# Where the moving operands lie: 256-byte offsets between weights and moving tiles in a hybrid decoder block

## The chip, the cores and the metric

The kernel runs on one core of a Trainium2 chip. The metric is the device time of one execution in microseconds; lower is better. Before the change three runs took 650.53, 650.55 and 651.75 us, a median of 650.55.

## What is computed

One decoder block on a sequence of 1024 tokens and a model width of 1024. After an RMS norm one projection feeds two groups of heads: eight heads of stick-breaking attention (head width 64) and four heads of a gated DeltaNet (head width 128). Both outputs are normed per head, gated, put side by side, and multiplied with one output matrix; the residual is added and normed once more. Cut to what matters here:

```python
h = rmsnorm(x, norm1_w)
proj = einsum('btd,de->bte', h, w_in)
sb_q, sb_k, sb_v, sb_z, g_q, g_k, g_v, g_z, g_b, g_a = split(proj)

# stick-breaking attention, strictly causal, per head
z = einsum('bhqd,bhkd->bhqk', sb_q, sb_k) / sqrt(64)        # scores
attn = where(causal, exp(log_sigmoid(z) - tail), 0)         # tail: sum of softplus(z) behind s
o_sb = rmsnorm(einsum('bhqk,bhkd->bhqd', attn, sb_v)) * silu(sb_z)

# gated delta rule in chunks, per head
o_gdn = rmsnorm(gated_delta_chunked(...)) * silu(g_z)

mixed = concatenate([o_sb, o_gdn], axis=-1)                 # 512 + 512 columns
x = x + einsum('bte,ed->btd', mixed, w_out)                 # output
return rmsnorm(x, final_norm_w)
```

All of it is float32. The change touches where the operands of two products lie, those named scores and output.

## The kernel before

**Products in three parts.** A wide product is made of three matmuls in the float32r type, on operands that are split into a high and a low part: high weights with the high moving operand, high weights with the low one, low weights with the high one (`mm3`, lines 586 to 589). The first argument after the output is the weights (stationary, 128 columns), the next is the moving operand, up to 512 columns. Each matmul instruction brings its own load of weights (LDWEIGHTS), and TensorE loads those of the next matmul while one streams. So the weights that are read during a matmul are those of the next one. In `mm3` two neighbours have the same high weights, and the third has the low ones.

**The stages.** The first stage computes q from the weights `wqh`, `wql` and the normed input `xh`, `xl` (lines 636 to 675). Then come v (`chl` is the moving operand there and `xh`, `xl` are the weights, lines 731 to 735 and 766 to 777), and the other projections (weights `weh`, `wel`, moving `xh`, `xl`, line 937). Attention and the delta rule are woven into the projections: a planner (`Model`, `interleave`) takes steps from several streams by their priorities and by estimated costs of operations, and what it records is the order on each engine. The order on PE is the order of recording. The estimates don't look at addresses.

**Scores.** For each head the planner's stream `attention` loads three tiles (lines 1261 to 1270): `q2` (the high and the low part of q on the two halves of the partitions), `kh` and `kl` (the high and the low part of k, each twice). A `window` then makes blocks of scores: the weights are a slice of 128 columns of `q2`, and `kh` and `kl` are the moving operands, in cuts of at most 512 columns (lines 1300 and 1301). The cuts and the slices begin at multiples of 128 columns, 512 bytes.

**Output.** `product` (lines 1461 to 1478) multiplies a block of 128 tokens, in `mh` and `ml` (the weights, four slices of 128 columns), with the scaled output matrix in `woh0` to `woh7` and `wol0` to `wol7` (moving, 512 columns at a time). It runs twice: first for the delta half (rows 4 to 7 of the matrix, whose tiles are in the pool `f0` on the left), and at the end for the attention half (rows 0 to 3, whose tiles are in the pool `f1` on the right), eight blocks each. The last block of the attention half is cut into 512, 320 and 192 columns.

**Memory.** SBUF is given out from two sides. On the left lie the fixed places (`sg0` to `sg3`, `o2`, `kq`), the constants, and above them, one after another in time, the pools `s0` (first stage), `gd` (delta rule) and `f0` (output). On the right, from the top downwards, lie `att` (attention's tiles, the lowest of which are `kh`, `kl`, `q2`, `v2a`), `pr` (the projections' weights), and under it `px` (`xh`, `xl`), later replaced by `f1`. A pool on the right ends where the one above it begins, so a pool that grows pushes down itself and all that lies under it. Several tags of `att` are used by `chl` tiles of 1040 floats at first, which makes their slots 4160 bytes where `kh` or `kl` need 4096.

The first bytes of the tiles in question, as the compiled program has them:

| tile | first byte | role |
|---|---|---|
| `q2` | 203488 | weights of scores |
| `kh` | 195168 | moving, scores |
| `kl` | 199328 | moving, scores |
| `mh` (three buffers) | 81280, 83328, 85376 | weights of output |
| `ml` (three buffers) | 87424, 89472, 91520 | weights of output |
| `woh4` | 54656 | moving, output, delta half |
| `woh0`, `wol0` | 133728, 137824 | moving, output, attention half |
| `weh` (three buffers) | 180832, 182880, 184928 | weights of the projections |
| `xh`, `xl` | 107104, 139872 | moving, projections |

The pool `gd` ends at byte 106944, 160 bytes below `xh`.

**Small tiles of the delta rule.** `gdn_pre` makes per unit (half a head) the columns `nk`, a root that ScalarE uses a little later (line 1070), and `qe`, which is used at the end of the unit's chain (line 1247).

Of the kernel before, what the change touches and what calls it, by code (L numbers as in the profile page):

```python
# [10 lines left out]
F32 = mybir.dt.float32  # L11
F32R = mybir.dt.float32r
# [5 lines left out]
P = 128  # L18
T = 1024
D = 1024  # L20
NB = T // P
NK = D // P
# [451 lines left out]
def block(tc, xT_d, x_d, n1_d, wE_d, wQ_d, wC_d, conv_d, alog_d, dtb_d, mixw_d, wo_d, fnw_d, out_d):  # L474
# [4 lines left out]
    with ExitStack() as top:  # L479
        top.enter_context(tc.manual_schedule(engines={mybir.EngineType.PE}))  # L480

        def open_pool(name, space="SB", ctx=top, before=(), **kw):
            if space != "SB":
                kw["space"] = getattr(bass.MemoryType, space)
            return Pool(ck, ctx.enter_context(tc.tile_pool(name=name, bufs=1, **kw)), space, before)

        fx = Fixed(ck, nc, {**{f"sg{w}": (2048 * (w + 1), 1) for w in range(4)}, "o2": (1024, 1), "kq": (4096, 4)})
# [52 lines left out]
        at_ = open_pool("att", side="right")  # L540
# [4 lines left out]
        xl = px.tile([P, NK, T], F32R, name="xl")  # L545
        s0_ctx = top.enter_context(ExitStack())
        s0 = open_pool("s0", ctx=s0_ctx)
        n1 = s0.tile([P, NK], F32, name="n1")
        rbc = s0.tile([P, T], F32, name="rbc")

        def turned(tp, parts):
# [65 lines left out]

        chl = []
        for tag, bufs in (("kh", 1), ("kl", 1), ("q2", 1), ("v2a", 1), ("sg2", 1), ("cc", 2), ("cc", 2), ("sg3", 1)):
            chl.append(fx.tile([P, 2, 520], F32R, "chl", tag) if tag[0] == "s" else at_.tile([P, 2, 520], F32R, tag=tag, bufs=bufs, name="chl"))  # L620
        sm = fx.tile([P, 768], F32, "sm", "sg1")
        ones, triu, zero = [sm[:, i * P:(i + 1) * P] for i in range(3)]
        ga = sm[:, 384:448].rearrange("p (b e) -> p b e", e=8)
# [132 lines left out]
        gd = open_pool("gd", ctx=gdn_ctx, before=s0.ops())  # L756
# [198 lines left out]
        def until(name):  # L955
            yield lambda: name in flags
            yield flags[name]


        def delta_pre():  # L960
            yield from decays(pre)
            for h in range(GH):
                for g in range(2):
                    u = 2 * h + g
                    yield from until(f"l{u}g")
                    yield from gdn_pre(h, g)
# [45 lines left out]
        def gdn_pre(h, g):  # L1012
            st = gst[h, g]
            kq = st["kq"]
            cs = slice(4 * g, 4 * g + 4)
            kn = gd.tile([P, 4, P], F32, tag="kn", bufs=4, name="kn")
            ss = gd.tile([P, 2, 4], F32, tag="ss", name="ss")
            cb = gd.tile([P, 4, P], F32, tag="cb", name="cb")
            S.dma_start(cb, cum_s[1, h, cs].partition_broadcast(P))
            dt = gd.tile([P, 4, P], F32, tag="dt", bufs=4, name="dt")  # L1020
            S.dma_start(dt, dt_s[h, g])

            nkv = gd.tile([P, 4, P], F32, tag="nkv", bufs=4, name="nkv")
            kw = fx.words(kq, "kw")
            for which in range(2):
                tp = pz()
                for j in range(4):
                    TE.transpose(tp[:, j * P:(j + 1) * P].bitcast(F32R), kw[:, j, which, :], idr)
                for j in range(4):
                    A.activation(nkv[:, j, :], tp[:, j * P:(j + 1) * P], AF.Square, accum_out=ss[:, which, j:j + 1])  # L1030
                sq = [("A", 250)] * 4
                if which == 0:
                    V.tensor_copy(kn.rearrange("p c d -> p (c d)"), tp)
                    yield
            G.tensor_scalar(ss, ss, EPS, None, ALU.add)
            r2b = gd.tile([P, 4], F32, tag="r2b", bufs=4, name="r2b")
            V.reciprocal(r2b, ss[:, 0, :])
            G.tensor_tensor(r2b, r2b, gsc["beta"][:, h, cs], ALU.mult)
            mr2b = gd.tile([P, 4], F32, tag="mr2b", name="mr2b")
            r = G.tensor_scalar(mr2b, r2b, -1.0, None, ALU.mult)  # L1040
            r2k = gd.tile([P, 4], F32, tag="r2k", bufs=4, name="r2k")
            G.tensor_tensor(r2k, r2b, gsc["kd"][:, h, cs], ALU.mult)
            nk = gd.tile([P, 4], F32, tag="nk", name="nk")
            G.tensor_tensor(nk, ss[:, 0, :], root, ALU.pow)
            qe = gd.tile([P, 4], F32, tag="qe", bufs=4, name="qe")
            G.tensor_scalar(qe, ss[:, 1, :], EPS * P, None, ALU.mult)
            yield r
            nm = dt
            at = gd.tile([P, 4, P], F32, tag="at", bufs=4, name="at")
            for i in range(2):  # L1050
                gpt = pz()
                for j in range(2):
                    c = 2 * i + j
                    TE.matmul(gpt[:, j * 256:(j + 1) * 256], kq[:, c, 0, :], kq[:, c, :, :].rearrange("p a t -> p (a t)"),
                              start=True, stop=True)
                gv = gpt.rearrange("p (j a t) -> p j a t", j=2, a=2)
                V.tensor_tensor(at[:, 2 * i:2 * i + 2, :], gv[:, :, 1, :], dt[:, 2 * i:2 * i + 2, :], ALU.mult)
                for j in range(2):
                    c = 2 * i + j
                    r = V.scalar_tensor_tensor(nm[:, c, :], gpt[:, j * 256:j * 256 + P], mr2b[:, c:c + 1], dt[:, c, :], ALU.mult, ALU.mult)  # L1060
                yield
            st.update(kn=kn, qe=qe, r2b=r2b, r2k=r2k, nkv=nkv, nm=nm, at=at)
            flags[f"p{2 * h + g}"] = r
            yield from until(f"v{2 * h + g}g")
            vt = st["vt"]
            tp = pz()
            for j in range(4):
                TE.transpose(tp[:, j * P:(j + 1) * P].bitcast(F32R), vt[:, j, :], idr)
            for j in range(4):
                A.activation(nkv[:, j, :], tp[:, j * P:(j + 1) * P], AF.Copy, scale=nk[:, j:j + 1])  # L1070
            qg = kq[:, :, 1, :]
            flags[f"q{2 * h + g}"] = G.tensor_tensor(qg, qg, cb, ALU.mult)
            yield
# [180 lines left out]
        def attention():  # L1254
            yield lambda: "v1" in flags and "dec" in flags
            for i in range(2):
                ccs.append(at_.tile([P, T + 1], F32, tag="cc", bufs=2, name="cc"))
                V.memset(ccs[i][:, T:T + 1], 0.0)
            for h in range(SBH):
                yield lambda: f"k{h // 2}" in flags  # L1260
                kh = at_.tile([P, T], F32R, tag="kh", name="kh")
                kl = at_.tile([P, T], F32R, tag="kl", name="kl")
                q2 = at_.tile([P, T], F32R, tag="q2", name="q2")
                i, r = h // 2, slice((h % 2) * 64, (h % 2) * 64 + 64)
                loads = []

                twice = lambda a: a[r, :].unsqueeze(1).to_broadcast([SBD, 2, T])
                for t, src in ((q2, qk_s[i, :, r, :].rearrange("n d t -> d n t")), (kh, twice(qk_s[4 + i, 0])), (kl, twice(qk_s[4 + i, 1]))):
                    loads.append(S.dma_start(t.bitcast(F32), src.bitcast(F32)))
                hd[h] = (q2, kh, kl)  # L1270
                yield loads
                for w in range(4):
                    tok = f"w{w}"
                    yield lambda: busy[tok] == 0 and len([1 for v in busy if v[0] == "w" and busy[v]]) < WINDOWS
                    busy[tok] = 1
                    yield Stream(window(h, w, tok), 10 + 0.01 * (4 * h + w), WINDOW + 0.01 * (4 * h + w))
                    yield lambda: f"s{h}{w}" in flags
            yield lambda: f"e{SBH - 1}3" in flags
# [88 lines left out]
        pools = {}  # L1367
# [145 lines left out]
        def products_attention():  # L1513
            yield lambda: f"d{NB - 1}" in flags
            for b in range(NB):
# [3 lines left out]
                for got in product(b, 0, parts):  # L1519
# [5 lines left out]
                        sy = pools[0].tile([P, 3], F32, tag="sy", bufs=2, name="sy")  # L1525
                        yf = block_tile(0, "yf") if last else y
                    V.tensor_tensor(y[:, hs], yp, y[:, hs], ALU.add)
                    junk = pools[1].tile([P, 512], F32, tag="yj", name="yj")
                    if n == 2:
                        V.scalar_tensor_tensor(junk[:, 0:hs.stop - hs.start], y[:, hs], 1.0 / D, y[:, hs], ALU.mult, ALU.mult, accum_out=sy[:, n:n + 1])  # L1530
                    else:
# [36 lines left out]
                    pre, Stream(delta_load(), 0.4, DELTA + 0.4), Stream(attention(), 9.995, WINDOW), Stream(attention_values(), 9.99, WINDOW), Stream(out_weights(), 9, OUT_WEIGHTS), Stream(out_weights_attention(), 9.25, OUTPUT + 1), Stream(enter_x(), 9.31, OUTPUT), fill,  # L1568
                    Stream(enter_delta(), 9.3, OUTPUT), Stream(prepare(1), 9.2, OUTPUT), Stream(products_delta(), 101, OUTPUT),
                    Stream(enter_attention(), 9.1, OUTPUT - 3), Stream(prepare(0), 9.05, OUTPUT - 2), Stream(products_attention(), 102, OUTPUT - 1.5)])  # L1570

        order = mybir.DependencyInfo(mybir.DependencyClass.NoSync, mybir.DependencyReason.DATA)
# [36 lines left out]
```

## Time and profile before

| | |
|---|---|
| median of three runs | 650.55 us |
| profiled execution | 650.36 us |
| its span, first to last instruction | 648.4 us |
| mean granted TensorE clock | 0.997 |
| matmul and weight-load instructions on PE | 3976 each |
| DMA | 111.82 MB, mean 172 GB/s |

The profile names operands by tiles, with buffer numbers left out, so that all eight `woh` tiles appear as `woh`; the two halves of the output are told apart by time (the delta half up to about 595 us, the attention half behind it). Nearly all operations carry line 358, that of the planner's recorder, so tiles are what tells groups apart. In the groups a matmul's busy time runs from its start to a modelled end, and neighbours overlap; the pace of a stream is read from the distance between starts.

### The profile page before, as it was taken

The numbers are of one execution on the slowest core, as the hardware profiler recorded it, in microseconds if no ns is written. First come the engines' busy times: TensorE is split into PE (matmuls) and PEld (weight loads), VectorE is DVE, ScalarE is ACT, GpSimd is POOL, SyncE is SP. The second block draws the span as 40 slices with busy tenths as digits, with TensorE's granted clock in tenths as the row PEclk, the third lists the DMA queues.
The fourth block names the chain that finished last, engine by engine and source line by source line (L and its number), as shares of the span: only waits on it lengthen the run. The fifth ranks groups of instructions, "written<-read, shape, count | busy, mean of one in ns | idle before, by whom it ended". The sixth has DMA issues, their size and how long they took to land.

```text
span 648.4 us, 11679 instructions
## 1 busy us (share of the span) xinstructions
PE 639.2 (99%) x3976; PEld 549.7 (85%) x3976; DVE 423.4 (65%) x779; ACT 393.7 (61%) x945; POOL 341.4 (53%) x428
## 2 busy tenths in 40 slices
PE   8999999999999999999999999999999999999996
PEld 7889989988888898888988878888888888888885
DVE  4469974223877869888528887457874326568874
ACT  6664577724967779876559786467854343043553
POOL 0115056837894678835479686287731223226642
PEclk9999999999999999999999999999999999999998
DMA  8976338865383446453463752725312259963312
GB/s 302 324 271 229 133 116 281 285 221 182 106 280 119 129 127 186 133 154 109 121 215 82 263 165 78 225 90 173 109 58 82 82 196 310 346 194 106 123 77 119
DMA packets 96666, 111.82 MB, mean 172 GB/s; under 512 B 28576, under 2 KB 61536, under 8 KB 96608
## 3 DMA queue, kind: packets, MB, share of 16 engines
q1 hardware_dynamic: 96320, 110.89, 52.4%
q8 instruction: 31, 0.51, 0.3%
q14 instruction: 27, 0.22, 0.1%
q10 hardware_dynamic: 288, 0.20, 0.1%
HBM read 76.03 MB, written 35.03 MB: 171 GB/s over the span
## 4 chain that ended last, share of the span: by engine, by line
PE 91%; DVE 4%; issue 1%; ACT 1%; POOL 1%; DMA 1%; POOLq 0%; SPq 0%; DVEq 0%; ACTq 0%
PE pp L358 55%; PE pz L358 26%; PE po L358 7%; PE pc L358 3%; DVE cc L358 1%; DMA kqf<-g_s 1%; ACT sgf L358 0%; DVE al L358 0%; DVE pp L358 0%; POOL sgf L358 0%; DVE wy L358 0%; DVE xr L358 0%; DVE ac L358 0%; POOL wel L358 0%; POOL ac L358 0%
## 5 line engine op out<-in xcount | busy, mean ns | idle before, releaser
L358 PE MATMUL pp<-xh,weh 128*128 128x512 f32 x360 | 150.3, 417 | 0.0
L358 PE MATMUL pp<-xh,wel 128*128 128x512 f32 x360 | 141.5, 393 | 0.0
L358 PE MATMUL pp<-xl,weh 128*128 128x512 f32 x360 | 141.0, 392 | 0.0
L358 POOL TENSOR_TENSOR wel<-wer,weh 128x512 fp32r<-128x512 f32 x48 | 62.8, 1314 | 86.1 <-ACT weh L358 69.7
L358 POOL TENSOR_TENSOR sgf<-sgf,cc 128x128 f32<-128x128 f32 (+3 forms) x64 | 77.3, 1210 | 50.4 <-DVE cc L358 45.0
L358 PEld LDWEIGHTS pp<-xh,wel 128*128 128x128 f32 x360 | 67.6, 188 | 15.2
L358 PEld LDWEIGHTS pp<-xl,weh 128*128 128x128 f32 x360 | 67.9, 189 | 8.6
L358 PEld LDWEIGHTS pp<-xh,weh 128*128 128x128 f32 x360 | 67.7, 188 | 8.7
L358 ACT ACTIVATE sgf<-pz,rs 128x384 f32<-128x384 f32 (+3 forms) x96 | 54.9, 606 | 7.5 <-PE pz L358 7.4
L358 DVE TENSOR_TENSOR_SCAN cc<-pz,step 128x384 f32<-128x384 f32 (+2 forms) x64 | 53.6, 847 | 8.9 <-ACT pz L358 7.4
L358 DVE TENSOR_TENSOR al<-pz,ah 128x512 fp32r<-128x512 f32 (+1 forms) x80 | 49.4, 628 | 13.3 <-ACT ah L358 12.9
L358 ACT ACTIVATE ah<-pz 128x512 fp32r<-128x512 f32 (+1 forms) x80 | 44.4, 572 | 21.0 <-PE pz L358 20.8
L358 ACT ACTIVATE pz<-pz,ns 128x384 f32<-128x384 f32 (+3 forms) x96 | 54.4, 585 | 0.0
L358 PE MATMUL pp<-woh,mh 128*128 128x512 f32 (+2 forms) x132 | 52.1, 394 | 0.0
L358 PE MATMUL pp<-woh,ml 128*128 128x512 f32 (+2 forms) x132 | 51.1, 387 | 0.0
L358 PE MATMUL pp<-wol,mh 128*128 128x512 f32 (+2 forms) x132 | 51.0, 386 | 0.0
L358 DVE SCALAR_TENSOR_TENSOR pp<-pre,conv,pp 128x512 f32<-128x512 f32 x42 | 31.5, 750 | 20.7 <-ACT pp L358 20.3
L358 POOL TENSOR_TENSOR ml<-mf,mh 128x512 fp32r<-128x512 f32 x16 | 22.1, 1380 | 41.2 <-ACT mh L358 35.6
L358 POOL TENSOR_TENSOR ac<-ac,pre 128x512 f32<-128x512 f32 x24 | 31.0, 1292 | 23.3 <-ACT pre L358 13.5
L358 PE MATMUL po<-ah,v2a 128*128 128x256 f32 (+1 forms) x160 | 41.9, 287 | 0.0
L358 DVE TENSOR_TENSOR_SCAN cc<-pz,cc,step 128x512 f32<-128x512 f32 (+1 forms) x32 | 38.8, 1212 | 2.8 <-ACT pz L358 2.4
L358 PE MATMUL po<-al,v2a 128*128 128x256 f32 (+1 forms) x160 | 38.8, 280 | 0.0
(292 smaller groups left out, 1591.8 us busy)
## 6 DMA issues: line engine op xcount, KB each, us to landing
wer<-wE SPq DMA_DIRECT2D x48, 256.0 KB, 3.8
xr<-x SPq DMA_DIRECT2D x16, 512.0 KB, 8.8
g_s<-ac SPq DMA_DIRECT2D x24, 256.0 KB, 2.5
v_s<-v2e SPq DMA_DIRECT2D x16, 256.0 KB, 2.7
kqf<-g_s SPq DMA_DIRECT2D x16, 256.0 KB, 5.3
v2a<-v_s SPq DMA_DIRECT2D x8, 512.0 KB, 5.0
q<-qk_s SPq DMA_DIRECT2D x8, 512.0 KB, 3.8
kh<-qk_s SPq DMA_DIRECT2D x8, 512.0 KB, 5.2
```

Of the source, the lines that this page charges most:

```text
L358: ins = f(*args, **kw).ins
```

## The change

Operations, their order and their data are the same. Five allocations differ:

- the second of the `chl` tiles, which shares the tag of `kl`, is 48 floats longer, so the slot of `kl` grows from 4160 to 4352 bytes;
- `kh` is taken as the columns from 16 on of a tile of 1040 floats, that is 64 bytes into its slot;
- `junk` (tag `yj`, a scratch output of the squares at the very end) is 584 floats wide and not 512;
- `n1` takes 24 floats and not 8, which moves the tiles behind it in `s0` up by 64 bytes;
- `nk` and `qe` become two halves of one tile with four buffers, which takes one slot of 32 bytes out of `gd`.

```diff
-        n1 = s0.tile([P, NK], F32, name="n1")
+        n1 = s0.tile([P, 24], F32, name="n1")[:, 0:NK]
...
         for tag, bufs in (("kh", 1), ("kl", 1), ("q2", 1), ("v2a", 1), ("sg2", 1), ("cc", 2), ("cc", 2), ("sg3", 1)):
-            chl.append(fx.tile([P, 2, 520], F32R, "chl", tag) if tag[0] == "s" else at_.tile([P, 2, 520], F32R, tag=tag, bufs=bufs, name="chl"))
+            if tag[0] == "s":
+                chl.append(fx.tile([P, 2, 520], F32R, "chl", tag))
+            else:
+                t = at_.tile([P, 1040 + (48 if tag == "kl" else 0)], F32R, tag=tag, bufs=bufs, name="chl")
+                chl.append(t[:, 0:1040].rearrange("p (a e) -> p a e", a=2))
...
-            nk = gd.tile([P, 4], F32, tag="nk", name="nk")
+            qn = gd.tile([P, 2, 4], F32, tag="qe", bufs=4, name="qn")
+            qe, nk = qn[:, 0, :], qn[:, 1, :]
             G.tensor_tensor(nk, ss[:, 0, :], root, ALU.pow)
-            qe = gd.tile([P, 4], F32, tag="qe", bufs=4, name="qe")
             G.tensor_scalar(qe, ss[:, 1, :], EPS * P, None, ALU.mult)
...
-                kh = at_.tile([P, T], F32R, tag="kh", name="kh")
+                kh = at_.tile([P, 1040], F32R, tag="kh", name="kh")[:, 16:1040]
...
-                    junk = pools[1].tile([P, 512], F32, tag="yj", name="yj")
+                    junk = pools[1].tile([P, 584], F32, tag="yj", name="yj")
```

## The prediction

> **What bounds the kernel now.** I read the page first, then a table of engine time by stage, then the chain of waits stage by stage, then single matmuls by their start times, and beside them the byte places of the operands.
>
> ```profile
> span 648.4 us, 11679 instructions
> PE 639.2 (99%) x3976; PEld 549.7 (85%) x3976; DVE 423.4 (65%) x779; ACT 393.7 (61%) x945; POOL 341.4 (53%) x428
> ...
> PE 91%; DVE 4%; issue 1%; ACT 1%; POOL 1%; DMA 1%; POOLq 0%; SPq 0%; DVEq 0%; ACTq 0%
> ```
>
> TensorE is the bound: it is busy 99% of the span, and 91% of the chain that ended last runs through it. The table by stage (columns: window, its length, then busy time and count of each engine, granted clock, DMA share, GB/s) says that this holds where the change works.
>
> ```profile
> 200.00:540.00 340.00, 338.98 (x2351) 292.98 (x2350) 231.09 (x421) 226.94 (x608) 200.15 (x269) 1.00 0.46 141
> 540.00:602.00 62.00, 62.00 (x298) 50.87 (x297) 40.30 (x78) 18.06 (x27) 22.16 (x16) 1.00 0.69 232
> 602.00:648.40 46.40, 40.29 (x196) 33.03 (x194) 30.29 (x56) 23.82 (x52) 20.49 (x20) 0.96 0.26 102
> ```
>
> In the attention stage PE rests 1.02 us of 340; in the first half of the output product it never rests; in the last stage it ends some 6 us before the span does, and what follows (evictions, a norm, the last stores) is as long whenever PE ends. A nanosecond taken from a matmul there is thus a nanosecond off the end, to within a tenth or so, as long as no other engine is made late. The question is only whether a matmul's time depends on where its operands lie.
>
> It seems to. By "offset" I mean the first byte of a moving operand minus the first byte of the weights that are loaded while it streams (those of the next matmul, which in these stages mostly lie in the same tiles as its own), modulo 256. In the output product the eight k-blocks come in two halves with the same weights tiles mh and ml, the same order and the same shapes. The delta half (weights rows 4 to 7) has offset 0, the attention half (rows 0 to 3) has 224: woh4 lies at byte 54656, woh0 at 133728, mh at 81280, and 512 or 2048 bytes from slice to slice change nothing. Here is one stretch of each half that no transpose interrupts, first and last of 13 starts, from the timeline of PE (start, duration, what):
>
> ```profile
> 580.45 0.39 PE L358 MATMUL pp<-woh,mh 128*128 128x512 f32 x1
> ...
> 583.17 0.39 PE L358 MATMUL pp<-woh,mh 128*128 128x512 f32 x1
> ```
>
> ```profile
> 633.45 0.40 PE L358 MATMUL pp<-woh,mh 128*128 128x512 f32 x1
> ...
> 636.25 0.40 PE L358 MATMUL pp<-woh,mh 128*128 128x512 f32 x1
> ```
>
> Twelve intervals: 2.72 us against 2.80, that is 226.7 ns a matmul at offset 0 and 233.3 ns at 224. The granted clock is 1.00 in the first window and 0.96 in the second, but the second's mean includes the time after PE ended, so I do not read a slower clock into it. The difference is not traffic either: the delta half has the larger DMA share (0.69 against 0.26) and is the faster. The projections, with xh at 107104 and weh at 180832 (offset 0), give a third sample, first and last of 20 starts:
>
> ```profile
> 150.21 0.39 PE L358 MATMUL pp<-xh,weh 128*128 128x512 f32 x1
> ...
> 154.52 0.39 PE L358 MATMUL pp<-xl,weh 128*128 128x512 f32 x1
> ```
>
> 4.31 us for 19 intervals, 226.8 ns. So two streams at offset 0 agree, and the one at 224 is 6.6 ns (3%) slower.
>
> **The change part by part.** No instruction is added or removed, no DMA, no wait is written. What moves, by the sizes: kl's slot grows by 192 bytes, so everything below it on the right side (kl, kh, the projection's weights and xh, xl) moves down 192; kh moves down 128, as its tile begins 64 bytes into the slot. q2 stays. kh minus q2 goes from offset 128 to 0, kl minus q2 from 192 to 0. The larger yj moves woh0 to wol3 down another 288, 480 in all: from 224 to 0. The other edits hold things still or make room: n1 moves the first stage's weights up 64 against xh's 192 down (256 together, offset still 0), and nk put beside qe frees the 32 bytes that xh needs. These two I cost at nothing: the same POOL instructions on the same sizes. nk now has four buffers rather than one, which only loosens its reuse; qe's reuse waits for a chain that the load of kq for the same unit has waited for already.
>
> *Output, attention half.* From the chain of waits (start, length, what):
>
> ```profile
> 560.22 5.55 PE pp L358 x24
> ...
> 566.06 5.57 PE pp L358 x24
> ...
> 571.92 5.56 PE pp L358 x24
> ...
> 577.78 11.00 PE pp L358 x48
> ...
> 592.20 4.95 PE pp L358 x21
> ...
> 597.44 4.96 PE pp L358 x21
> ...
> 602.69 4.26 PE pp L358 x18
> ...
> 607.25 5.67 PE pp L358 x24
> ...
> 613.21 5.67 PE pp L358 x24
> ...
> 619.18 5.67 PE pp L358 x24
> ...
> 625.15 14.08 PE pp L358 x60
> ```
>
> A block of 24 behind its transposes takes 5.56 us at offset 0 and 5.67 at 224: 0.11 us, or 4.6 ns a matmul, less than 6.6 because the first ten or so after a switch run slower in both halves. Three such blocks: 0.33. The pieces of 21 and 18, with nine of the piece at 592.20: 48 x 4.6 ns = 0.22. The last piece, 60 without a break, takes 14.08; at offset 0 it would take 11.00 for 48 and 12 x 226.7 ns = 2.72 for the rest, 13.72: 0.36. Together 0.91 us. The last block's 24 narrow matmuls (320 and 192 wide) are not in it; at the same 3% the 320 wide ones would bring 12 x 4 ns, 0.05, and the 192 wide ones nothing, as the load of 188 ns is longer than their streaming. I take 0.95; bounds 0 (if the halves differ for another reason) and 180 x 6.6 ns = 1.2.
>
> *Scores.*
>
> ```profile
> L358 PE MATMUL pz<-kh,q 128*128 128x512 f32 x40 | 17.6, 441 | 0.1
> L358 PE MATMUL pz<-kl,q 128*128 128x512 f32 x40 | 15.7, 393 | 0.0
> ...
> L358 PE MATMUL pz<-kh,q 128*128 128x384 f32 x24 | 9.0, 375 | 0.4 <-DVE al L358 0.4
> ...
> L358 PE MATMUL pz<-kh,q 128*128 128x256 f32 x24 | 8.0, 333 | 0.1
> ```
>
> Each kh matmul streams while the same q2 slice is loaded once more for kl: all 96 change offset as asked. The kl ones mostly stream while the next stream's weights are loaded, and meet q2 only 33 times by the program's order. Of the 40 wide kh matmuls, by their starts, 19 run on without a hitch, at 235 ns on average (229 to 241), and 21 take 284 or more, since they stand behind a switch of streams where the load is on the path. The first kind would gain some 7 ns, 0.13 us; 13 of the 384 wide run on at 177 where 384/512 of 226.7 is 170, 0.09; 8 of the 256 wide at 120 against 113, 0.05; the kl ones that meet q2, 0.08. That is 0.35. The 53 behind a switch I give a fifth of their 6 ns, 0.05, because the delta half's first interval behind its transposes is no shorter than the attention half's (0.31 us between 565.89 and 566.20, and the same between 619.01 and 619.32):
>
> ```profile
> 565.89 0.46 PE L358 MATMUL pp<-woh,mh 128*128 128x512 f32 x1
> 566.20 0.39 PE L358 MATMUL pp<-wol,mh 128*128 128x512 f32 x1
> ```
>
> ```profile
> 619.01 0.47 PE L358 MATMUL pp<-woh,mh 128*128 128x512 f32 x1
> 619.32 0.40 PE L358 MATMUL pp<-wol,mh 128*128 128x512 f32 x1
> ```
>
> Scores: 0.40 us, bounds 0 and 0.75 (all of them in full).
>
> *What moves along.* xh and the projection's weights change offset against all that stays (q2, v2a, kq, xinv, the transposed tiles): about 170 wide matmuls at the ends of projection steps. The gdn tiles behind nk move 32 bytes, some 550 small float32 matmuls, and six of the eight chl tiles stay while xh moves, 288 matmuls. Few of them sit at offset 0, before or after. The chl ones go round among the same offsets in steps of 64, so their sum stays, and their rows show little to gain anyway:
>
> ```profile
> L358 PE MATMUL pz<-chl,xh 128*128 128x264 f32 x48 | 9.3, 287 | 0.0
> ...
> L358 PE MATMUL pp<-chl,xh 128*128 128x264 f32 x24 | 4.6, 285 | 0.0
> ```
>
> I take 0 for all of them, with bounds of 0.5 us either way (170 x 3 ns, half of the 6.6).
>
> Sum: 0.95 + 0.40 = 1.35 us off the profiled execution's 650.36 gives 649.0. The median of the runs, 650.55, is 0.19 above the profiled one, so against the runs the forecast is **649.2**.
>
> **A rule that speaks against it.** The Trainium skill, page "SBUF — State Buffer", section "Who interferes with whom", gives TensorE two independent read ports, one for the moving operand and one for weights, and says that "PE and ACT never wait on anyone". By it no offset could matter and the time would stay at 650.55. The 226.7 against 233.3 ns above do not agree with it as it stands, unless something else sets the two halves apart; so it is a rival below.
>
> **The rivals.**
> *Nothing moves.* The halves would differ by something that I have not seen, say by ACT's and DVE's reads: ACT is busy 18.06 of 62 us in the delta half's window and 23.82 of 46.4 in the last. Against it: the projections run at 226.8 in a third stage with other neighbours, and the attention half keeps its pace to the last block, where fewer and fewer other operations stand beside it. Time 650.5.
> *Only the output gains.* The score matmuls stand so often behind a switch that the load, not the stream, sets their pace (21 of the 40 wide ones). Then 0.95 is all: 649.6.
> *More gains.* If those behind a switch gain in full and a few of the moved ends happen to be aligned: 0.95 + 0.75 + 0.3 = 2.0, 648.5.
> *Slower.* The 192 bytes put xh, xl and the projection's weights at new offsets to everything left in place, and the 32 bytes do it to the gdn chain: 170 + 100 short loads for the projection + 288 + 550, some 1100 matmuls whose offsets come out as they may. If the new offsets cost 2.7 ns more each on average, 3.0 us, the kernel ends at 652.2. It decides from 1.2 ns each (1.35 us over 1100). For it: the number is large and an offset of 224 is worth 6.6 ns. Against: they were unaligned before too, and the small float32 ones stream at half the pace and leave room.
>
> **How the numbers follow.** A measurement of this kernel can tell about 0.2%, 1.3 us, from no change: below 649.25 is faster, above 651.85 slower. The forecast's case, both gains at roughly their size (-0.95 to -1.8), 0.62; it straddles the bound, and I put 0.40 of it beyond, as the terms taken were the cautious ones, and 0.22 within. More gains 0.10, faster. Only the output 0.08 and nothing 0.08, both within. Slower 0.12. So faster 0.50, same 0.38, slower 0.12. The range from 648.2 to 650.9 leaves out the slower case and a little of the largest gain; it takes in the bounds of the moved ends. The forecast's own range is 648.7 to 649.6.
>
> **What would show it.** In the profile after: a stretch of the attention half's output without transposes at 226.7 ns a matmul (12 intervals in 2.72 us), the blocks of 24 in the chain at 5.55 rather than 5.67, the last piece of 60 at 13.7; kh's steady intervals at 227 to 229 and its 512 wide mean below 441; delta half and projections as before. The prediction is wrong if the attention half still runs at 233, if the wide matmuls at the ends of projection steps or the gdn chain's got longer by more than a nanosecond on average, or if PE's rest in the attention stage grows over its 1.02 us.

## The result, and the profile after

The changed kernel takes 649.64 us (median of 19 runs, 648.96 to 650.83) against 650.55 before (19 runs, 649.78 to 651.75): 0.91 us or 0.14% less, a ratio of 0.9985 with a 95% interval of 0.9978 to 0.9992. The ratios here and below are taken over undisturbed runs and are not the quotients of the medians. So it is faster than before, but by less than the 0.2% that the prediction set as its bound. The profiled execution took 649.73 us. The page of the changed kernel, the rows that answer to those of before:

```profile
span 647.8 us, 11679 instructions
PE 637.6 (98%) x3976; PEld 548.5 (85%) x3976; DVE 423.8 (65%) x779; ACT 394.5 (61%) x945; POOL 341.1 (53%) x428
...
PE 92%; DVE 3%; ACT 2%; DMA 1%; issue 1%; SPq 0%; POOL 0%; POOLq 0%; DVEq 0%; ACTq 0%
```

The same instructions, PE's in the same order, and 1.6 us less of PE's busy time. Where it went is seen in the chain of waits of the changed kernel from 540 us on (start, length, what), the pieces of the output product:

```profile
560.44 5.55 PE pp L358 x24
...
566.29 5.55 PE pp L358 x24
...
572.13 5.57 PE pp L358 x24
...
578.00 11.00 PE pp L358 x48
...
592.43 4.87 PE pp L358 x21
...
597.60 4.89 PE pp L358 x21
...
602.78 4.19 PE pp L358 x18
...
607.26 5.57 PE pp L358 x24
...
613.12 5.60 PE pp L358 x24
...
619.02 5.57 PE pp L358 x24
...
624.88 13.72 PE pp L358 x60
```

Up to the piece of 48 (the delta half) nothing has changed. From the piece at 592 on each is shorter: 5.57 to 5.60 for 5.67, 4.19 for 4.26, and 13.72 for 14.08. The stretch without transposes, first and last of 13 starts in PE's timeline of the changed kernel:

```profile
632.99 0.39 PE L358 MATMUL pp<-woh,mh 128*128 128x512 f32 x1
...
635.71 0.39 PE L358 MATMUL pp<-woh,mh 128*128 128x512 f32 x1
```

2.72 us for 12 intervals, 226.7 ns a matmul, where there were 233.3. The scores, by group, in the changed kernel:

```profile
L358 PE MATMUL pz<-kh,q 128*128 128x512 f32 x40 | 17.5, 438 | 0.1
L358 PE MATMUL pz<-kl,q 128*128 128x512 f32 x40 | 15.8, 394 | 0.0
...
L358 PE MATMUL pz<-kh,q 128*128 128x384 f32 x24 | 8.9, 373 | 0.4 <-DVE al L358 0.4
...
L358 PE MATMUL pz<-kh,q 128*128 128x256 f32 x24 | 7.9, 330 | 0.1
```

kh's means fell by 2 or 3 ns (441 to 438, 375 to 373, 333 to 330), kl's rose by 1 to 3 (393 to 394, 335 to 338, 279 to 280). These means say little by themselves. In e2_output, a kernel from further below in which no score tile is moved, the first of them is no higher:

```profile
L358 PE MATMUL pz<-kh,q 128*128 128x512 f32 x40 | 17.5, 437 | 0.1
```

As PE's order is the same in both traces, the distance from each start to the next can be set against its counterpart. Summed by class, in us:

| class | matmuls | before | after | difference |
|---|---|---|---|---|
| output, attention half | 203 | 45.38 | 44.55 | -0.84 |
| output, delta half | 192 | 44.45 | 44.46 | +0.01 |
| scores, kh | 96 | 21.19 | 20.92 | -0.28 |
| scores, kl followed by q2 | 33 | 6.28 | 6.37 | +0.09 |
| scores, kl followed by others | 63 | 12.11 | 12.21 | +0.10 |
| projections, weights after weights | 981 | 234.38 | 234.20 | -0.19 |
| projections, other weights next, offset moved | 170 | | | +0.17 |
| chl, offset moved | 288 | | | -0.29 |
| first stage | 192 | | | +0.37 |
| all others | | | | +0.21 |

The differences add up to 0.63 us, which is also that between the two profiled executions (650.36 and 649.73). The first stage's +0.37 lies at its first weights: the chain of the changed kernel's execution has a wait for the DMA of `wq` there (1% of the span) that the other's does not show. It comes and goes: in the eleven kernels below the first stage is 0.07 to 0.72 above before. The -0.29 of chl does not. It returns as -0.28 or -0.29 in the four kernels below that contain the same move (e1, e3, e5, e6), and the five that leave these tiles and `xh` alone (e2, e4, e9, e10, e11) lie at -0.01 to -0.04. What the runs' 0.91 is made of is settled by edits.

### The profile page after: what moved, and what is told of

It is laid out like the page before. It is cut to its first block, busy times and chain, and to the rows that moved or that the text cites. A ratio compares the mean times of both kernels' runs of the same rounds, so it can differ in the third digit from the quotient of the medians.

```text
span 647.8 us, 11679 instructions
## 1 busy us (share of the span) xinstructions
PE 637.6 (98%) x3976; PEld 548.5 (85%) x3976; DVE 423.8 (65%) x779; ACT 394.5 (61%) x945; POOL 341.1 (53%) x428
## 4 chain that ended last, share of the span: by engine, by line
PE 92%; DVE 3%; ACT 2%; DMA 1%; issue 1%; SPq 0%; POOL 0%; POOLq 0%; DVEq 0%; ACTq 0%
PE pp L358 56%; PE pz L358 26%; PE po L358 7%; PE pc L358 3%; DMA wq<-wQ 1%; DVE cc L358 1%; ACT nkv L358 0%; ACT sgf L358 0%; DVE al L358 0%; SPq L358 0%; DVE wy L358 0%; DVE xr L358 0%; ACT ah L358 0%; DVE pp L358 0%; DVE wc L358 0%
```

## Experiments

All kernels compute the same, with PE's instructions in the same order; only tiles lie elsewhere. "Offset" is used as in the prediction. The first four of the table were timed against the kernel before on one chip, the fifth on another; the kernels that it does not list are read from one profiled execution each.

| kernel | time, us | before on the same chip | ratio, 95% interval |
|---|---|---|---|
| e1_scores | 650.72 | 650.99 | 0.9999, 0.9990 to 1.0008 |
| e2_output | 650.02 | 650.99 | 0.9986, 0.9977 to 0.9995 |
| e3_delta_off | 650.62 | 650.99 | 0.9997, 0.9989 to 1.0006 |
| e7_proj_off | 654.59 | 650.99 | 1.0056, 1.0042 to 1.0070 |
| e8_values | 650.35 | 651.22 | 0.9985, 0.9975 to 0.9994 |

**The output alone.** One edit to the kernel before moves woh0 to wol3 by 224 bytes:

```diff
-                    junk = pools[1].tile([P, 512], F32, tag="yj", name="yj")
+                    junk = pools[1].tile([P, 568], F32, tag="yj", name="yj")
```

> The kernel before with one edit: the scratch tile yj is 568 floats wide, which moves the attention half's weights matrix by 224 bytes to offset 0; nothing else moves. Theory: the last piece of 60 takes 13.72 us, blocks of 24 take 5.56; total 0.85 us below before, 649.7, that is nearly all that the whole change brought (0.91). Rival (moves of other tiles carry a good part of the gain): less than 0.5 us, above 650.05. Rival (the offset plays no part): 650.55, piece of 60 at 14.08.

The ratio is 0.9986, that of the whole change (0.9985). Its chain of waits:

```profile
607.82 5.55 PE pp L358 x24
...
625.39 13.73 PE pp L358 x60
```

The attention half's intervals add up to 44.52, against 45.38 before: 0.87 us. A scratch tile that is written and never read, made 56 floats wider, brings nearly all of it; the rival that other moves carry the gain falls. Here `woh0` lies 52224 bytes above `mh`, 204 times 256; in the changed kernel it is 51968, 203 times 256. Both have the short interval, so a distance that differs by 256 bytes counts as the same.

**The scores without the output.** The changed kernel, all its other moves included, with the scratch tile at 528 floats, by which the attention half is back at offset 224:

```diff
-                    junk = pools[1].tile([P, 584], F32, tag="yj", name="yj")
+                    junk = pools[1].tile([P, 528], F32, tag="yj", name="yj")
```

> The change with the score tiles moved as in it, but the scratch tile yj only 528 floats wide, so that the attention half of the output lies at offset 224 again (as before). Theory (the offset to the weights loaded meanwhile sets the pace): the attention half of the output runs at 233 ns a matmul as before, its last piece of 60 in the chain takes 14.08 us; the steady kh intervals are 227 to 231; total 0.2 to 0.4 us below before, 650.2 to 650.4 (in the changed kernel all kh and kl intervals that meet q2 were 0.18 us shorter in sum). Rival (only the output gains, the scores bring nothing): 650.5, kh 512 wide mean busy time still about 441 ns.

The time can't be told from before (0.9999, and 0.27 us between the medians). The chain's last piece is long again:

```profile
625.50 14.09 PE pp L358 x60
```

kh's intervals add up to 20.94 and those of all 96 kl to 18.57. Which part of that is the move is seen across all kernels, as the execution shown for before has the largest kh sum of those that leave the scores alone (sums in us, lowest to highest):

| intervals | scores moved (five kernels) | not moved (eight, with before) |
|---|---|---|
| kh, 96 | 20.91 to 20.96 | 21.07 to 21.19 |
| kl, 96 | 18.47 to 18.59 | 18.36 to 18.43 |
| both | 39.42 to 39.54 | 39.42 to 39.58 |

kh did gain, 0.19 us between the means, and kl lost 0.16: together 0.03, less than either group spreads. The steady 512 wide kh matmuls take 229.5 to 229.9 ns where the scores are moved and 232.6 to 235.1 where they are not; before's 235.1 is the highest.

**The delta half made worse.** The changed kernel, with mh and ml moved by 32 bytes:

```diff
-            fv = pools[0].tile([P, 512], F32, tag="mf", name="mf")
+            fv = pools[0].tile([P, 520], F32, tag="mf", name="mf")[:, 0:512]
...
-                    junk = pools[1].tile([P, 584], F32, tag="yj", name="yj")
+                    junk = pools[1].tile([P, 640], F32, tag="yj", name="yj")
```

> The changed kernel with the scratch tile mf 32 bytes larger, which moves mh and ml by 32 bytes, so that k-blocks 4 to 6 of the delta half of the output get offset 224; k-block 7 and the attention half (moved along by a wider yj) stay at offset 0. Theory: in the delta half the uninterrupted intervals become 233 ns in k-blocks 4 to 6 and stay 227 in k-block 7, about 144 x 4.6 ns = 0.65 us more than the changed kernel, 650.3. Rival (the halves differ by their neighbours, not by offset): no change against the changed kernel, 649.64.

Its chain of waits, two pieces of the delta half, then the last of the attention half:

```profile
561.22 5.66 PE pp L358 x24
...
579.08 11.23 PE pp L358 x48
...
626.25 13.73 PE pp L358 x60
```

The halves have changed places: 5.66 in the delta half, and the attention half as short as ever. The delta half's intervals grew from 44.46 to 45.15, 0.69 us (0.65 expected), and the time lies 0.60 above e2_output's. What set the two halves apart was the offset and not their neighbours. Nor was it where one operand lies by itself: here the weights moved, in e2_output the moving tiles. One thing did not fit: in k-block 7, still at offset 0, the intervals were 233, 230 and 229 ns on average and not 227.

**The projections made worse.** The kernel before, xh and xl moved by 64 bytes:

```diff
-        n1 = s0.tile([P, NK], F32, name="n1")
+        n1 = s0.tile([P, 56], F32, name="n1")[:, 0:NK]
...
-                    r = pr.tile([P, 512], F32, tag="wer", bufs=2, name="wer")
+                    r = pr.tile([P, 520], F32, tag="wer", bufs=2, name="wer")[:, 0:512]
...
-                    junk = pools[1].tile([P, 512], F32, tag="yj", name="yj")
+                    junk = pools[1].tile([P, 560], F32, tag="yj", name="yj")
```

> The kernel before with the raw weights tiles wer 32 bytes larger each, which moves xh and xl by 64 bytes, so that all projections get offset 192 where they had 0 (981 matmuls of 512 columns between projection weights); the first stage's weights and the attention half of the output are moved so that they keep their offsets. Theory: the steady projection intervals go from 227 to 230 to 233 ns; some 800 steady ones x 3 to 6.6 ns = 2.4 to 5.3 us slower, 653 to 656. Rival (only the output stage is sensitive): 650.55, projection intervals at 227.

3.6 us slower (654.59 against 650.99). The stretch that the prediction showed for the projections, first and last of 20 starts in this kernel's timeline:

```profile
149.99 0.40 PE L358 MATMUL pp<-xh,weh 128*128 128x512 f32 x1
...
154.42 0.39 PE L358 MATMUL pp<-xl,weh 128*128 128x512 f32 x1
```

4.43 us for 19 intervals, 233.2 ns for 226.8. In all five stretches of over 50 projection matmuls the mean behind the first dozen went from 226.7 to 233.3 or 233.4. Over all 981 the intervals grew by 4.2 us, 4.3 ns each: in the shorter stretches less was lost, which again says that a matmul at offset 0 does not always have the short interval. The 171 projection matmuls that other weights follow became 0.44 us shorter, a part of why the runs lost 3.6 and not 4.2.

**Whose weights.** The output's edit, and only ml moved by 32 bytes:

```diff
-                mh, ml = [pool.tile([P, 4, P], F32R, tag=f"m{c}", bufs=3, name=f"m{c}") for c in "hl"]
+                mh = pool.tile([P, 4, P], F32R, tag="mh", bufs=3, name="mh")
+                ml = pool.tile([P, 576], F32R, tag="ml", bufs=3, name="ml")[:, 8:520].rearrange("p (k t) -> p k t", k=4)
```

> The kernel before with yj 568 floats wide (attention half at offset 0) and the ml tiles moved by 32 bytes while mh stays. Each k-step has three matmuls: mh with woh, mh with wol, ml with woh; the weights loaded meanwhile are mh, ml, mh. Theory (the weights loaded meanwhile count): in uninterrupted stretches of both halves the second, wol with mh, slows to about 233 ns (offset 224 to ml) and the other two stay at 227. Rival (the weights that the moving operand is multiplied with count): the third, woh with ml, slows to 233, and the second stays at 227. Rival (any of the two): both slow.

Distances between starts in one uninterrupted run of twelve matmuls of the delta half, the same place in three kernels (ns, in the order mh·woh, mh·wol, ml·woh):

```
before       227 226 227 227 226 227 227 226 227 227 226 227
e4_ml_off    232 239 229 232 239 229 232 239 229 232 239 229
e3_delta_off 233 234 232 235 232 234 233 234 232 234 231 226
```

The second matmul of the three, during which ml is loaded, is by far the slowest (239), and the third, which multiplies with ml, the least slow (229). So it is the load of ml, and not the product with it, that goes with the longest interval. But both other matmuls, at offset 0 to what they load, are slower than 226.7 too, and the three together take 700 ns, as much as if all were off (699.9 for three at 233.3). One disturbed matmul of three costs as much as three.

**Offsets by k-block.** Pads between the tiles of the attention half's matrix (this is e5_scan_a; e6_scan_b has 16, 8 and 8 floats and yj at 528):

```diff
-                wh, wl = [pool.tile([P, D], F32R, name=f"wo{c}{k}") for c in "hl"]
+                wh, wl = [pool.tile([P, D + ({0: 8, 1: 8, 2: 16}.get(k, 0) if c == "l" else 0)], F32R, name=f"wo{c}{k}")[:, 0:D] for c in "hl"]
...
-                    junk = pools[1].tile([P, 584], F32, tag="yj", name="yj")
+                    junk = pools[1].tile([P, 552], F32, tag="yj", name="yj")
```

> The changed kernel with pads between the tiles of the attention half's matrix, so that k-blocks 0 to 3 lie at offsets 0, 32, 64 and 128 (both woh and wol). Theory: only offset 0 gives 227 ns in uninterrupted stretches, the other three 230 to 234. Rival (what counts is a coarser or finer step, 128 or 64 bytes): k-block 3, or k-blocks 2 and 3, also at 227.

> The same with offsets 96, 160, 192 and 224 in k-blocks 0 to 3. Theory: all four between 230 and 234 ns, 224 at 233. Rival (the distance from a multiple of 256 counts, 32 bytes either way being the worst or the mildest): 96 and 160 differ from 224 by more than 3 ns.

Neither could settle its question. Distances in one uninterrupted half each:

```
e5_scan_a (0, 32, 64, 128)     235 233 236  229 236 234  237 230 231  232 232 228
e6_scan_b (96, 160, 192, 224)  230 237 231  232 228 231  234 236 231  236 232 227
```

No k-block of the first runs at 227, not even the one at offset 0, and within a block of three the values differ more than between blocks. Three matmuls between others don't show what an offset is worth. e6's k-blocks average 230 to 234 ns, as its theory had it, but so do three of e5's, the one at offset 0 averages 235, and so e6 decides nothing. The theory that each interval depends on its own offset alone was no longer tenable, and the next kernels asked about whole streams and about what follows a disturbance.

**Whole streams.** The kernel before, the offsets set by the sizes of mf and yj (544 and 520 floats in e9, 560 and 512 in e10):

```diff
-            fv = pools[0].tile([P, 512], F32, tag="mf", name="mf")
+            fv = pools[0].tile([P, 544], F32, tag="mf", name="mf")[:, 0:512]
...
-                    junk = pools[1].tile([P, 512], F32, tag="yj", name="yj")
+                    junk = pools[1].tile([P, 520], F32, tag="yj", name="yj")
```

> The kernel before with mf 128 bytes larger and yj 520 floats wide: the delta half's k-blocks 0 to 2 lie at offset 128 (its k-block 3 stays at 0), the whole attention half at 64. So each offset holds for a whole stream, not for one k-block of three matmuls between others. Theory A (any offset but 0 slows a whole stream): 230 to 234 ns in both, as at 224. Theory B (the pace depends on the offset modulo 128 or 64): the delta half's blocks 0 to 2 at 227, at 64 bytes also the attention half.

> The same with the delta half's k-blocks 0 to 2 at offset 64 and the whole attention half at 32. Theory A: 230 to 235 ns in both. Theory B (modulo 64): the delta half's at 227, the attention half's slow.

The last three uninterrupted halves of the attention half take 2.746 and 2.747 us at offset 64 and 2.800 at 32, as at 224; 2.720 at 0. So 228.9 ns at 64, 233.3 at 32. In the chain of e9:

```profile
626.13 13.84 PE pp L358 x60
```

13.84 between 13.72 and 14.08. Neither theory was right: 32 and 224 cost 6.6 ns, 64 costs 2.2, and it is not modulo 64, or the stream at 64 would have been at 227. In the delta half, with k-block 7 at 0 in each run of 12, both kernels ran at 225 to 241 ns in no steady pattern, 2.77 to 2.80 us a half; its intervals add up to 0.66 us more than before with three k-blocks at 128 and 0.47 with them at 64. A whole stream at 128, 96 or 160 was not tried.

**Behind a disturbance.** The output's edit, and of the delta half only the first k-block 32 bytes off:

```diff
-                wh, wl = [pool.tile([P, D], F32R, name=f"wo{c}{k}") for c in "hl"]
+                wh, wl = [(pool.tile([P, D + 64], F32R, name=f"wo{c}{k}")[:, 8:D + 8] if k == 4 else
+                           pool.tile([P, D], F32R, name=f"wo{c}{k}")) for c in "hl"]
```

> The kernel before with the attention half at offset 0 and only the first k-block of the delta half (woh4, wol4) at offset 32; so in each run of 12 matmuls three are off and nine at 0. Theory C (a stream at offset 0 needs some ten matmuls to come to 226.7 ns after each disturbance, as behind the transposes): the nine are slow too at first, 229 to 236, and come down to 227 towards the end of the 12; the uninterrupted halves take about 2.77 to 2.80 us in place of 2.72. Rival (each interval depends on its own offset alone): three at 233, nine at 227, 2.74 us.

One uninterrupted half in the timeline of this kernel, from its first start to that of the next half:

```profile
581.24 0.40 PE L358 MATMUL pp<-woh,mh 128*128 128x512 f32 x1
...
581.94 0.39 PE L358 MATMUL pp<-woh,mh 128*128 128x512 f32 x1
...
584.00 0.40 PE L358 MATMUL pp<-woh,mh 128*128 128x512 f32 x1
```

2.766 us by the exact starts, and 2.766 to 2.775 in seven of the eight halves that no transpose precedes (2.778 in the first): theory C. Its distances, beside a half behind transposes in the kernel before:

```
e11, three off, then nine at 0   236 230 236  230 236 228 233 231 226 227 227 226
before, behind transposes        303 229 233 236 224 231 236 228 233 231 226 227
```

The off matmuls are the first three. The five that follow lie at offset 0 and are slow all the same, and they end in the same steps as those behind the transposes: 236, 228, 233, 231, and only then 226 and 227. Both kinds of disturbance are worked off over some five to ten matmuls. What is worked off there, no run shows.

**The values too.** The kernel before with the output's edit and, besides, v2a moved so that ah and al meet it at offset 0:

```diff
-            chl.append(fx.tile([P, 2, 520], F32R, "chl", tag) if tag[0] == "s" else at_.tile([P, 2, 520], F32R, tag=tag, bufs=bufs, name="chl"))
+            if tag[0] == "s":
+                chl.append(fx.tile([P, 2, 520], F32R, "chl", tag))
+            else:
+                t = at_.tile([P, 1040 + (8 if tag == "cc" else 0)], F32R, tag=tag, bufs=bufs, name="chl")
+                chl.append(t[:, 0:1040].rearrange("p (a e) -> p a e", a=2))
...
-                    junk = pools[1].tile([P, 512], F32, tag="yj", name="yj")
+                    junk = pools[1].tile([P, 552], F32, tag="yj", name="yj")
```

(n1 is 56 floats wide here, for the first stage's offset.)

> The kernel before with the attention half of the output at offset 0 and, in place of the scores, the moving operands ah and al of attention times values at offset 0 to v2a (they had 192): the slots of the cc tiles grow by 32 bytes each, and the first stage's weights keep their offset. 249 matmuls of mostly 256 columns meet v2a. Theory: a 256 wide matmul takes 118 ns before; if the offset costs 3% there too, 114 ns and 249 x 4 ns = 1.0 us less than the output's edit alone, 648.7. Rival (a matmul of 256 columns is paced by the load of its successor's weights, not by its stream): 118 ns as before, 649.7.

No gain: the ratio is 0.9985, e2_output's is 0.9986. The 256 wide matmuls had a median distance of 118 ns and now 119; over all that meet v2a it went from 30.34 us to 30.57 (30.30 to 30.46 in the other kernels). Why a 256 wide stream doesn't care here was not separated: the rival's reason, the pace of loading, fits, but the 256 wide kh matmuls did gain (119 to 120 not moved, 114.5 to 115.5 moved, in their eight steady cases).

## Why the prediction was right or wrong

The forecast was 649.2 and the time is 649.64; direction and range held. The range, 648.2 to 650.9, says little by that: it holds the time before, too. The narrower one, 648.7 to 649.6, was missed by 0.04, and the likeliest outcome, faster by over 0.2% at 0.50, did not come. The gain is two thirds of the one predicted, and of the terms of the sum one was sized well and one was not.

*The bound.* Right. PE's order did not change, its savings went through to the end, and no other engine became late. From the table by stage of the changed kernel:

```profile
200.00:540.00 340.00, 338.87 (x2352) 293.00 (x2351) 231.56 (x420) 227.28 (x608) 200.51 (x269) 1.00 0.46 141
```

PE rests 1.13 us of 340 in the attention stage where it rested 1.02. By the letter that is one of the signs of being wrong that the prediction named, a rest that grows; but the other eleven kernels lie between 1.00 and 1.11, so 0.11 is within what the order of events in one execution brings.

*The output, 0.95.* Right in mechanism and nearly in size: 0.84 in the changed kernel, 0.87 in e2_output. The last piece came out at the 13.72 that the prediction had computed as 11.00 + 2.72. The blocks behind transposes gave 0.10, 0.07 and 0.10 rather than 0.11 each. Of the narrow ones the 320 wide brought 0.01, not 0.05. The 192 wide brought nothing, as forecast, but not for the reason given: they follow one another at 112 ns before and after, well below the 188 that the prediction took for the limit. The step that inferred the cause from two halves of one product was shown by e3_delta_off, where the halves change places.

*The scores, 0.40.* Here the sum went wrong: by the means of the thirteen kernels they brought 0.03. The kh part, put at 0.32, was 0.19. The matmuls behind a switch, given 0.05 of that, gained nothing that shows (the 21 of 512 columns take 6.69 to 6.70 us moved, 6.60 to 6.72 not). The step that failed most is "the kl ones that meet q2, 0.08": those lost 0.09 (6.31 to 6.40 us in the five kernels that moved them, 6.24 to 6.28 in the eight that did not). The 63 other kl, left out of the sum, lost another 0.06, though for most of them the weights loaded meanwhile (`weh`) moved along with `kl`. The prediction treated each matmul as if its own offset alone set its time. e4, e5 and e11 show that this fails: a matmul at offset 0 has the short interval only after a run of undisturbed ones, and kh and kl come in pairs, between streams with other weights. That fits kh, too: its steady 512 wide ones fell to 229.5 and not to 226.7. What makes kl slower, and not merely no faster, stays open; the five kernels share all other moves of the change, so it need not be the scores' own.

*What moves along, 0 within 0.5 either way.* Held within the bound, but not at 0. chl gained about 0.26, in all five kernels with this move: shifting its offsets by 64 bytes did not leave the sum as it was. The ends of projection steps show +0.17 in the one execution, which is 1.0 ns a matmul and so at the sign of being wrong; over the five kernels they take 42.54 to 42.67 us, in the six that leave their offsets alone 42.48 to 42.70, so nothing is seen. The delta rule's 424 matmuls on `xinv`, `kqf`, `v` and `at` take 43.91 to 43.96 us in the five and 43.83 to 43.92 in the other eight, about 0.1 ns more each, far from a nanosecond. What the scores did not bring, chl made up for in part, and that was luck.

*The rivals.* The time came out at that of "only the output gains" (649.6), within the 0.2%, for nearly that reason: kh gained, kl lost as much, and chl added a little that the rival had not counted. The reason it gave, that the load sets the pace behind a switch, fits those matmuls; the steady kh gained, and kl took it back. It had been given 0.08, and the forecast's own case had been centred on the very bound of 0.2%, with too much of it beyond. "Nothing moves" falls with e2, e3 and e7. The Trainium skill (page "SBUF — State Buffer", section "Who interferes with whom") gives TensorE separate read ports for the moving operand and for weights and calls them independent. A move of 64 bytes that costs 3.6 us does not agree with that, if it is read as the prediction did, that no offset could matter. The sentence that the prediction quotes from there is about engines that wait on one another; what was moved here are two operands of one engine, and no run tests it. "Slower" and "more gains" did not happen.

## What to carry to other kernels

Where TensorE is the bound and wide float32r matmuls follow one another, look at the byte offset between a moving operand and the weights that are loaded while it streams, modulo 256: in a long run offset 0 gave 226.7 ns and 32, 192 or 224 gave 233.3, and a pad in a scratch tile can set it. Count on the gain only for long runs: in the short, alternating streams of the scores kh gained 0.19 us and kl lost 0.16, and one misplaced tile among aligned ones, or a switch of streams, slows the next five to ten matmuls as well. And an edit elsewhere that moves a pool by 32 bytes can take 3% from a stream that nobody touched, so compare offsets before explaining a small loss by the edit itself.

## What the runs showed of the hardware that was not expected

- A stream at offset 0 settles: distances of 229 to 236 ns come down in the same steps (236, 228, 233, 231, 226) to a repeating 227, 226, 227, behind transposes as behind three misplaced matmuls.
- One matmul in three whose successor's weights lie 32 bytes off costs as much (700 ns for three) as all three being off (699.9).
- The cost is not the same for all offsets: 2.2 ns at 64, 6.6 at 32, 192 and 224, for 512 columns.
